# Where the largest entry of a weight strip is taken over the partitions: by a library call on GpSimd, or through DRAM and VectorE

## The chip, the cores and the metric

The kernel runs on one core of one Trainium2 chip. The metric is the time of one execution in microseconds of the device, as the median of several runs. The core has five engines that run side by side, each with its own queue of instructions in a fixed order: TensorE (PE, with its weight loads shown apart as PEld), VectorE (DVE), ScalarE (ACT), GpSimd (POOL) and SyncE (SP), which in this kernel issues most of the transfers. The engines wait for each other by semaphores, and an instruction that waits holds up all that stand behind it on its engine.

## The reference

One inference step of a decoder with two layers, width 1024, on 1040 prompt positions (16 of them meta tokens) and 8 single new tokens. Cut to what matters:

```python
def trunk(x, ...):
    for i in range(2):
        h = rms_norm(x, norm_mix_pre[i])
        m = ssd_mixer(h, ...) if i == 0 else rglru_mixer(h, ...)
        x = x + rms_norm(m, norm_mix_post[i])
        h = rms_norm(x, norm_ffn_pre[i])
        x = x + rms_norm((relu(h @ w1[i]) ** 2) @ w2[i], norm_ffn_post[i])

def ssd_chunked(xdt, a, Bm, Cm, h0, chunk):      # 8 groups of 4 heads of 64, state 128
    cb = einsum("bclgn,bcsgn->bcgls", Cc, Bc)
    scores = cb[:, :, :, None] * Lmat            # Lmat = exp(segment sums), lower triangle
    y_diag = einsum("bcgrls,bcsgrp->bclgrp", scores, x)
    chunk_states = einsum("bcsgn,bcsgrp->bcgrpn", Bc, x * decay_to_end[..., None])
    ...                                          # scan over the chunks, y_off, states out
```

`ssd_mixer` stands between `w_in` (1024 x 6176) and `w_out` (2048 x 1024), `rglru_mixer` between 1024 x 2048 and 1024 x 1024, and each feed-forward part has a `w1` of 1024 x 4096 and a `w2` of 4096 x 1024. All inputs and outputs are float32.

## The kernel before

Everything is kept with the features on the 128 partitions and the tokens along the free axis, in three pieces of about 350 tokens. A product of float32 matrices is made of three float16 products: weights and activations are each split into a high and a low half. For that a weight has to be scaled first by a power of two that comes from its largest entry, and this is done in the kernel, strip by strip.

**The strips.** The weights arrive in strips of 128 partitions x 2048 float32 (1 MB each), 109 of which are scaled as follows. `wlane` (L400) is a generator that issues the load of strip i+1 (`load_strip`, L258, two buffers) and then converts strip i (`wconv`, L286): the largest absolute value of each partition goes to `rm` (128 x 1; on ScalarE for the strips of kind "a", on VectorE for the others), `strip_scale` (L263) makes one number of the 128 and a power of two from it, and `split` (L272) writes the two float16 halves into `wh`, ScalarE the high one, VectorE the low one. Strips of the kinds "H" and "S" (feed-forward) also need sums of their quarters: `sums` (L350) first splits three quarters into `wp` and then lets GpSimd add quarters in place (`ws<-ws`). In `strip_scale` the maximum over the partitions is one GpSimd call, `partition_all_reduce`, which leaves it in all 128 partitions of `wgb`; behind it VectorE makes the power of two in three operations on 128 x 1 (`qw`, `pw`, `sw`, in `pow2`, L246) and its inverse (`winv`). The profile shows 105 of the 109 calls; two more calls of the kind, for other small tables, stay as they are.

**The stages**, in the times of the profiled execution: the start (0 to 133 us: inputs, first norm, first strips; its order is held by hand as written), the eight groups of the state-space layer (`ssd_group`, L985, some 95 us each, to 880 us), its output product (to 1100), the first feed-forward part (to 1715), the recurrent layer (to 2130), and the second feed-forward part, whose last product with the output ends at 2886 us.

**Feed-forward.** Three of the four blocks of `w1` and of `w2` are multiplied by a scheme with seven products of quarters in place of eight (`unit`, L1342). The products of a unit land in four PSUM tiles, and while PE makes the next, VectorE adds them up in an SBUF tile `z`. In front of the products stand sums of the right-hand quarters: for the input `input_sums` (L1324, tiles `f`, written to `TT`), for the hidden layer `square` (L1231) and `t_sums` (L1311): ScalarE squares, GpSimd makes four sums in place (`z<-z`, or `r<-r`), ScalarE and VectorE split them into `HT`. So in the feed-forward GpSimd has two kinds of work in one queue: sums for the activations (`z`, `f`), on which PE's next products depend, and the maxima and sums of the coming weight strips (`wgb`, `ws`).

**State-space groups.** Per group nine chunks are worked off in a loop (L1124): `spread` (L1012) issues, on SP, the broadcast of the cumulative sums (`L<-csd`) and of their exponentials (`ex<-esd`), `pe_a` (L1004) puts three transposes and the product of B and C into one PSUM tile `tp`, `ew_a` (L1026) reads that tile (VectorE: `xdt`, `xdd`, `cbm`; ScalarE: the copy `Bt`) and makes the decay matrix `L`, `pe_b` (L1046) multiplies, and `ew_b` (L1062) gathers. `tri` is the mask of the lower triangle.

**What sets the order.** The program is written as interleaved generators (`tick` lets each lane run one step), and a scheduler then orders each engine's queue, from its own costs and from which tiles' buffers come free. Only the start is held in the written order. Nearly every operation goes through one helper, so most rows of the profile carry its line, L89 (L92 in the start); operations are told apart by their tiles.

Of the kernel before, what the change touches and what calls it, by code (L numbers as in the profile page):

```python
# [10 lines left out]
F32 = mybir.dt.float32  # L11
# [3 lines left out]
OP = mybir.AluOpType  # L15
AX = mybir.AxisListType
PSUM = bass.MemoryType.PSUM
DRAM = bass.MemoryType.DRAM
RED = bass.bass_isa.ReduceOp
EXPSET = "natural_log_exp_and_others"  # L20

P = 128
# [95 lines left out]
class Body:  # L118
# [34 lines left out]
    def setup(self):  # L153
        nc, tc, ctx = self.nc, self.tc, self.ctx
        self.const = ctx.enter_context(tc.tile_pool(name="const", bufs=1))
        self.tiny = ctx.enter_context(tc.tile_pool(name="tiny", bufs=3))
        self.upool = ctx.enter_context(tc.tile_pool(name="u", bufs=1))
        self.ws = ctx.enter_context(tc.tile_pool(name="ws", bufs=2))
        self.wh = ctx.enter_context(tc.tile_pool(name="wh", bufs=5))
# [30 lines left out]
        gb = c.tile([P, 5], F32, name="gb")  # L190
# [18 lines left out]
        self.yd = [self.dram.tile([P, 4 * NV], F16, name=f"yd{i}") for i in range(G)]  # L209
        self.csd = self.dram.tile([288, P], F32, name="csd")  # L210
        self.esd = self.dram.tile([288, P], F32, name="esd")
        self.bcd = [self.dram.tile([8, 2, P], F32, name=f"bcd{i}") for i in range(2)]
        self.mad = [self.dram.tile([P, KT * w], F32, name=f"mad{c}") for c, w in enumerate(WC)]
        a = self.a
# [46 lines left out]
        return st  # L261

    def strip_scale(self, gmax):  # L263
        nc, ty = self.nc, self.tiny
        gb = ty.tile([P, 1], F32, tag="wgb", name="wgb")
        nc.gpsimd.partition_all_reduce(gb, gmax, P, RED.absmax)
        s, p = self.pow2(gb, 1, ty, "w")
        inv = ty.tile([P, 1], F32, tag="winv", name="winv", bufs=8)
        nc.vector.tensor_scalar(inv, p, 2.0 ** -14, None, op0=OP.mult)
        return s, inv, gb  # L270
# [714 lines left out]
    def ssd_group(self, g):  # L985
        nc, v, psp, tmp = self.nc, self.v, self.psp, self.tmp
# [5 lines left out]
        ident, tri = self.ident, self.tri  # L992
# [6 lines left out]
        def dims(i):  # L999
            if i == 0:  # L1000
                return 16, 8, slice(32, 48), 8
            return 128, i - 1, slice(48 + 128 * (i - 1), 176 + 128 * (i - 1)), 24 + 128 * (i - 1)
# [23 lines left out]
        def ew_a(i, tp):  # L1026
            Q, tt, es, _ = dims(i)
            xdt = tmp.tile([P, 4, 64], F32, tag="xdt", name="xdt", bufs=2)
            xdd = tmp.tile([P, 4, 64], F32, tag="xdd", name="xdd", bufs=2)
            L = S.pop(("L", i))  # L1030
            for h in range(4):
                nc.scalar.activation(L[:Q, h, :Q], L[:Q, h, :Q], AF.Relu, scale=-1.0,
                                     bias=self.cs[:Q, tt, 4 * g + h:4 * g + h + 1])
            self.tab(L[:Q, :, :Q], L[:Q, :, :Q], AF.Exp, scale=-1.0)
            tv = tp[:Q, :256].rearrange("p (h d) -> p h d", h=4)
            nc.vector.tensor_tensor(xdt[:Q], tv, self.dt[:Q, tt, hs, None].to_broadcast([Q, 4, 64]), op=OP.mult)
            nc.vector.tensor_tensor(xdd[:Q], tv, self.dtd[:Q, tt, hs, None].to_broadcast([Q, 4, 64]), op=OP.mult)
            Bt = tmp.tile([P, 128], F32, tag="Bt", name="Bt", bufs=2)
            nc.scalar.activation(Bt[:Q], tp[:Q, 256:384], AF.Copy)
            cbm = tmp.tile([P, 128], F32, tag="cbm", name="cbm", bufs=2)  # L1040
            nc.vector.tensor_tensor(cbm[:Q, :Q], tp[:Q, 384:384 + Q], tri[:Q, :Q], op=OP.mult)
            nc.vector.tensor_tensor(L[:Q, :, :Q], L[:Q, :, :Q], cbm[:Q, None, :Q].to_broadcast([Q, 4, Q]),
                                    op=OP.mult)
            S[i] = xdt, xdd, L, Bt
# [79 lines left out]
        for i in range(n + 1):  # L1124
            if i + 1 < n:
                spread(i + 1)
            if i:
                rb = pe_b(i - 1)
            if i < n:
                ra = pe_a(i)  # L1130
            if i:
                ew_b(i - 1, *rb)
            if i < n:
                ew_a(i, ra)
            if i == 1:
                sample_bc()
                sample_a()
            if i in (3, 4, 5, 6):
                sample_b(i - 3)
            if i == 8:  # L1140
                sample_c()
            yield
# [508 lines left out]
```

## Time and profile before

| | |
|---|---|
| median of 3 runs | 2877.12 us (2875.55 to 2878.47) |
| the profiled execution, its own time | 2887.62 us |
| its span in the trace | 2885.9 us |
| mean granted clock of TensorE | 0.96 |
| PE busy | 2571.2 us (89%), 23193 matmuls |
| VectorE busy | 2050.4 us (71%) |
| ScalarE busy | 1403.1 us (49%) |
| GpSimd busy | 743.0 us (26%) |
| transfers | 237.71 MB, 82 GB/s in the mean |

How to read it: the profiled execution is 10.5 us longer than the median of the runs, and 1.7 us of its time lie outside the span. Busy time is time in which an instruction of the engine runs; an instruction that waits for a semaphore is not busy. In a timeline each row has the start (us from the span's start), the busy time of the instructions it stands for, the engine, the line, the operation with its output and inputs, and in brackets how long the engine was idle just before and what ended that. In the list of waits the three numbers are the total, the number of times and the longest, in us. "issue" as a releaser means that the engine waited for nothing that the profile shows. A view by windows gives, for each stretch, its length, the busy time of each engine with the number of instructions, the granted clock of TensorE (1.00 is full speed), the share of the transfer engines and the GB/s moved.

### The profile page before, as it was taken

To read this page: it belongs to the slowest core of one execution; us is meant where nothing else is said; L and a number is where in the kernel's file an instruction comes from. 1 tells how busy PE (TensorE), PEld (TensorE's weight loads), DVE (VectorE), ACT (ScalarE), POOL (GpSimd) and SP (SyncE) were. 2 spreads that over 40 slices of the span, in tenths; PEclk is the share of its full clock that TensorE was granted. 3 is DMA by queue.
4 is the path that set the end of the run, shared out by engine and by line. 5 is a ranking of instruction groups with operands and counts; after the bars stand their busy time and mean duration, and the time that the engine had idled before them with its cause. 6 is when DMAs were issued, how large, how long until landed. Compare 5 with 4: busy or idle time off the path is not lost. (4 is left out here: it accounts for less than half of the span.)

```text
span 2885.9 us, 57203 instructions
## 1 busy us (share of the span) xinstructions
PE 2571.2 (89%) x23193; PEld 2025.2 (70%) x23193; DVE 2050.4 (71%) x4682; ACT 1403.1 (49%) x2436; POOL 743.0 (26%) x1036
## 2 busy tenths in 40 slices
PE   4988998899897999878989999988999879989998
PEld 2655665565565666777988986665666879979976
DVE  4878666766862596567878788787695567777776
ACT  4666565665654355335244253567564335244342
POOL 2233222212222103543232210223012543231201
PEclk9999999999999999989999999999999989999999
DMA  3333233223344330011112122210130011111122
GB/s 125 96 119 127 73 127 119 97 93 119 125 151 164 132 144 30 30 34 42 60 60 89 45 96 96 96 68 33 70 124 30 31 45 45 45 45 45 60 72 93
DMA packets 71496, 237.71 MB, mean 82 GB/s; under 512 B 11120, under 2 KB 37152, under 8 KB 50368
## 3 DMA queue, kind: packets, MB, share of 16 engines
q1 hardware_dynamic: 64848, 199.35, 20.3%
q0 software_dynamic: 6384, 34.71, 3.1%
q8 instruction: 181, 2.97, 0.4%
q14 instruction: 83, 0.68, 0.1%
HBM read 194.67 MB, written 39.36 MB: 81 GB/s over the span
## 5 line engine op out<-in xcount | busy, mean ns | idle before, releaser
L89 PEld LDWEIGHTS <-wh 128*128 128x128 f16 x17040 | 1499.2, 99 | 516.3 <-issue 59.8
L89 PE MATMUL mm<-U,wh 128*128 128x350 f16 (+3 forms) x7056 | 993.2, 297 | 20.1 <-ACT rr L89 10.2
L89 PE MATMUL mm<-H,wh 128*128 128x175 f16 (+5 forms) x5664 | 557.4, 253 | 37.0 <-DVE z L89 33.0
L89 PEld LDWEIGHTS <-wp 128*128 128x128 f16 x3888 | 310.8, 99 | 91.1 <-issue 63.9
L89 POOL TENSOR_TENSOR ws<-ws 128x256 f32<-128x256 f32 (+1 forms) x192 | 205.0, 1068 | 328.7 <-DVE wp L89 214.2
L89 DVE TENSOR_TENSOR z<-z,mm 128x175 f32<-128x175 f32 (+3 forms) x648 | 228.4, 370 | 28.9 <-ACT z L89 22.0
L89 POOL PARTITION_ALL_REDUCE wgb<-rm x100 | 50.3, 503 | 683.2 <-issue 296.6
L89 PE MATMUL mm<-U,wp 128*128 128x175 f16 (+1 forms) x1728 | 154.8, 245 | 56.0 <-DVE z L89 51.9
L89 PE MATMUL mm<-TT,wh 128*128 128x175 f16 (+1 forms) x1728 | 164.7, 246 | 9.8 <-ACT TT L89 8.9
L89 ACT ACTIVATE z<-z,ti 128x700 f32<-128x700 f32 (+1 forms) x72 | 63.0, 875 | 184.7 <-DVE z L89 184.7
L89 DVE SCALAR_TENSOR_TENSOR wh<-ws,sw,wh 128x1024 f16<-128x1024 f32 x94 | 127.0, 1368 | 34.0 <-ACT wh L89 34.0
L89 DVE TENSOR_SCALAR qw<-wgb 128x1 f32<-128x1 f32 x103 | 15.5, 151 | 187.0 <-POOL wgb L89 187.0
L89 ACT ACTIVATE L<-L,cs 128x128 f32<-128x128 f32 (+1 forms) x288 | 92.3, 380 | 109.2 <-DMA L<-csd 90.2
L89 DVE SCALAR_TENSOR_TENSOR conv<-pre,ssmall,conv 128x1072 f32<-128x1072 f32 x78 | 120.3, 1543 | 9.6 <-ACT conv L89 9.2
L89 DVE SCALAR_TENSOR_TENSOR wh<-ws,s,wh 128x256 f16<-128x256 f32 x256 | 114.6, 490 | 11.1 <-ACT wh L89 11.1
L89 PE MATMUL mm<-H,wp 128*128 128x175 f16 (+1 forms) x864 | 91.3, 243 | 27.8 <-DVE z L89 22.5
L89 DVE TENSOR_REDUCE rm<-ws 128x1 f32<-128x2048 f32 x40 | 91.3, 2282 | 28.4 <-DMA ws<-w 24.5
L89 ACT ACTIVATE wh<-ws,sw 128x2048 f16<-128x2048 f32 x47 | 93.7, 1995 | 34.6 <-DVE sw L89 27.8
L89 ACT ACTIVATE wh<-ws,s 128x512 f16<-128x512 f32 x128 | 83.0, 710 | 48.6 <-POOL ws L89 23.4
L89 DVE TENSOR_TENSOR ss<-ss,sqt 128x350 f32<-128x350 f32 (+3 forms) x154 | 75.8, 499 | 41.9 <-ACT sqt L89 41.5
L89 DVE TENSOR_TENSOR H<-z,H 128x175 f16<-128x175 f32 (+5 forms) x120 | 82.5, 705 | 22.5 <-ACT H L89 18.4
L89 POOL TENSOR_TENSOR yf<-yf,ex 128x256 f32<-128x256 f32 x64 | 51.4, 803 | 177.4 <-issue 86.1
(274 smaller groups left out, 4134.6 us busy)
## 6 DMA issues: line engine op xcount, KB each, us to landing
ws<-w SPq DMA_DIRECT2D x64, 1024.0 KB, 4.9
ws<-w_ssd_in SPq DMA_DIRECT2D x24, 1024.0 KB, 5.0
L<-csd SPq DMA_DIRECT2D x64, 256.0 KB, 3.5
ws<-w_lru_in SPq DMA_DIRECT2D x12, 1024.0 KB, 5.1
xd<-xc POOLq DMA_DIRECT2D x6, 1400.0 KB, 5.1
xc<-xd SPq DMA_DIRECT2D x6, 1400.0 KB, 5.9
h<-ssd_h SPq DMA_DIRECT2D x8, 1024.0 KB, 5.3
ex<-esd SPq DMA_DIRECT2D x128, 64.0 KB, 3.9
```

What stands on the lines that cost most here:

```text
L89: r = f(*args, **kw)
```

## The change

In `strip_scale` the GpSimd call is replaced by four steps: SP writes `rm` (128 numbers) to one of four small DRAM tensors `mxd`; SP reads it back as a row of 128 that is broadcast to all partitions (`wrow`, 128 x 128, one buffer); VectorE takes the maximum along the row into `wgb`; the rest follows as before. The pool of the small tiles has 2 buffers in place of 3 (among them `rm` and `wgb`). In `ew_a` VectorE's `cbm` now stands ahead of ScalarE's `Bt`; both read the same PSUM tile `tp`.

```diff
-        self.tiny = ctx.enter_context(tc.tile_pool(name="tiny", bufs=3))
+        self.tiny = ctx.enter_context(tc.tile_pool(name="tiny", bufs=2))
...
+        self.mxd = [self.dram.tile([P, 1], F32, name=f"mxd{i}") for i in range(4)]
+        self.nmax = 0
...
     def strip_scale(self, gmax):
         nc, ty = self.nc, self.tiny
+        d = self.mxd[self.nmax % 4]
+        self.nmax += 1
+        nc.sync.dma_start(d, gmax)
+        row = ty.tile([P, P], F32, tag="wrow", name="wrow", bufs=1)
+        nc.sync.dma_start(row, d.rearrange("p o -> o p").to_broadcast([P, P]))
         gb = ty.tile([P, 1], F32, tag="wgb", name="wgb")
-        nc.gpsimd.partition_all_reduce(gb, gmax, P, RED.absmax)
+        nc.vector.tensor_reduce(gb, row, axis=AX.X, op=OP.max)
         s, p = self.pow2(gb, 1, ty, "w")
...
             nc.vector.tensor_tensor(xdd[:Q], tv, self.dtd[:Q, tt, hs, None].to_broadcast([Q, 4, 64]), op=OP.mult)
+            cbm = tmp.tile([P, 128], F32, tag="cbm", name="cbm", bufs=2)
+            nc.vector.tensor_tensor(cbm[:Q, :Q], tp[:Q, 384:384 + Q], tri[:Q, :Q], op=OP.mult)
             Bt = tmp.tile([P, 128], F32, tag="Bt", name="Bt", bufs=2)
             nc.scalar.activation(Bt[:Q], tp[:Q, 256:384], AF.Copy)
-            cbm = tmp.tile([P, 128], F32, tag="cbm", name="cbm", bufs=2)
-            nc.vector.tensor_tensor(cbm[:Q, :Q], tp[:Q, 384:384 + Q], tri[:Q, :Q], op=OP.mult)
```

The scheduler then orders all queues anew. Three places show what moves. The first is GpSimd's queue in the first feed-forward part, at the first hidden blocks: `ws` are the sums of a strip's quarters, `wgb` the maximum, `z` the sums for the hidden layer. Before:

```order
L89 TENSOR_TENSOR ws<-ws 128x4x128 x4
L89 ISA
L89 ISA wgb<-rm 128x1
L89 ISA
L89 TENSOR_TENSOR z<-z 128x175 x8
L89 TENSOR_TENSOR z<-z 128x174 x4
L89 TENSOR_TENSOR ws<-ws 128x4x128 x4
L89 TENSOR_TENSOR z<-z 128x175 x4
```

And with the change:

```order
L89 TENSOR_TENSOR ws<-ws 128x4x128 x4
L89 TENSOR_TENSOR z<-z 128x175 x8
L89 TENSOR_TENSOR z<-z 128x174 x4
L89 TENSOR_TENSOR ws<-ws 128x4x128 x4
L89 TENSOR_TENSOR z<-z 128x175 x8
L89 TENSOR_TENSOR z<-z 128x174 x4
L89 TENSOR_TENSOR ws<-ws 128x2x128 x16
L89 TENSOR_TENSOR ws<-ws 128x4x128 x12
```

The call and the two nameless instructions at its sides are gone from all 109 places, so that sums follow sums; GpSimd's queue goes from 852 rows to 503.

The second place is VectorE's queue in the first feed-forward part at a strip of `w2`: `rm` is the strip's maximum by partition, `qw` the first operation behind the maximum over the partitions, `z` and `H` work for the products. Before:

```order
L89 TENSOR_TENSOR H<-z,H 128x2x350
L89 TENSOR_TENSOR z<-mm,z 128x2x175
L89 TENSOR_TENSOR r4s<-r_14617,rj 128x4
L89 TENSOR_TENSOR z<-z,mm 128x175
L89 TENSOR_REDUCE rm<-r4s 128x1
L89 TENSOR_TENSOR z<-z,mm 128x2x175
L89 TENSOR_TENSOR z<-z,mm 128x175
L89 TENSOR_TENSOR z<-z,mm 128x174
L89 TENSOR_SCALAR qw<-wgb 128x1
```

And with the change:

```order
L89 TENSOR_TENSOR H<-z,H 128x2x350
L89 TENSOR_REDUCE rm<-r4s 128x1
L89 TENSOR_TENSOR z<-mm,z 128x2x175
L89 TENSOR_TENSOR z<-z,mm 128x175
L89 TENSOR_TENSOR z<-z,mm 128x2x175
L89 TENSOR_TENSOR z<-z,mm 128x175
L89 TENSOR_REDUCE wgb<-wrow 128x1
L89 TENSOR_SCALAR qw<-wgb 128x1
```

Four operations stand between `rm` and the next step, which is now a reduction that waits for a transfer; before it were three, and the wait was for GpSimd.

The third place is SP's queue in a group of the state-space layer: `ws<-w_ssd_in` are strip loads, `L<-csd` and `ex<-esd` the broadcasts for the chunks, `bcd` and `bc` a round trip through DRAM that both kernels have. Before:

```order
L260 DMA ws<-w_ssd_in 128x2048
L1023 DMA ex<-esd 64x2x128 x2
L1018 DMA L<-csd 128x512
L260 DMA ws<-w_ssd_in 128x2048 x2
L1023 DMA ex<-esd 64x2x128 x2
L1018 DMA L<-csd 128x512 x2
L1087 DMA bcd_145<-row 8x256
L1090 DMA bc<-bcd_145 128x2048
```

And with the change:

```order
L1004 DMA h_4154<-ssd_h 128x2048
L262 DMA ws<-w_ssd_in 128x2048
L1026 DMA L<-csd 16x4x16
L1031 DMA ex<-esd 64x2x128 x2
L1026 DMA L<-csd 128x512
L270 DMA mxd_146<-rm 128x1
L1031 DMA ex<-esd 64x2x128 x2
L272 DMA wrow<-mxd_146 128x128
L262 DMA ws<-w_ssd_in 128x2048 x2
L1026 DMA L<-csd 128x512 x2
```

The write and the read of each strip's maximum stand between the broadcasts and ahead of the next strips' loads; SP's queue goes from 217 rows to 518. VectorE's goes from 3825 to 3955.

## The prediction

> **What bounds the kernel now.** The page's first part, its chain of work and one of its costliest groups come first.
>
> ```profile
> PE 2571.2 (89%) x23193; PEld 2025.2 (70%) x23193; DVE 2050.4 (71%) x4682; ACT 1403.1 (49%) x2436; POOL 743.0 (26%) x1036
> ...
> DVE 7%; issue 4%; PE 4%; DMA 2%; ACT 1%; POOL 1%; DVEq 0%; SPq 0%; POOLq 0%; ACTq 0%
> ...
> L89 POOL PARTITION_ALL_REDUCE wgb<-rm x100 | 50.3, 503 | 683.2 <-issue 296.6 <-DVE rm L89 200.7 <-ACT rstd L89 53.0
> ```
>
> PE is busy for 89% of the span, so some 315 us are left in which it is not. GpSimd is busy for 26%, and yet it matters: a maximum over the partitions runs 503 ns, but 296.6 us of idle time before these calls are "issue", time for which the profile shows no cause. The waits say how that is spread.
>
> ```profile
> POOL wgb L89 <- issue: 296.6, 48, 9.4
> ...
> DVE qw L89 <- POOL wgb L89: 187.0, 75, 11.2
> ...
> PE mm L89 <- DVE z L89: 113.1, 70, 6.2
> ...
> POOL ws L89 <- issue: 96.8, 14, 10.3
> ...
> POOL yf L89 <- issue: 86.1, 12, 7.6
> ...
> POOL f L89 <- issue: 56.8, 8, 7.7
> ```
>
> 48 calls stand behind 6.2 us each (296.6/48), and ordinary sums behind a call (`ws`, `yf`, `f`) behind 6.9, 7.2 and 7.1 us. GpSimd seems to change its code on the way into the call and on the way back: 13 us for half a microsecond of work. Whether PE feels it is seen in a feed-forward place in the timeline:
>
> ```profile
> 1472.46 0.41 POOL L89 PARTITION_ALL_REDUCE wgb<-rm  x1 [6.10 <-issue]
> 1472.90 0.15 DVE L89 TENSOR_SCALAR qw<-wgb 128x1 f32<-128x1 f32 x1 [4.49 <-POOL wgb L89]
> 1473.85 1.08 PE L89 MATMUL mm<-U,wp 128*128 128x175 f16 x12 [1.50 <-DVE z L89]
> ...
> 1479.64 4.08 POOL L89 TENSOR_TENSOR z<-z 128x175 f32<-128x175 f32 x8 [6.78 <-DVE wh L89]
> ...
> 1486.14 0.33 DVE L89 TENSOR_TENSOR z<-z,mm 128x175 f32<-128x175 f32 x1
> 1486.52 1.90 PE L89 MATMUL mm<-U,wp 128*128 128x174 f16 x12 [5.81 <-DVE z L89]
> ```
>
> VectorE stands 4.49 us at `qw`, which costs PE 1.50. The way back costs more: the sums of `z` start 6.78 us after the call (put down to `wh`, but the same length as "issue" above), `z` comes late, PE stands 5.81 us. There are 14 such places, where GpSimd goes from a call straight to sums of `z` or `f`. Cut out as windows, the first, the last and the sum of the 14; then of four stretches between them in which everything runs:
>
> ```profile
> 1198.00:1220.00 22.00, 15.34 (x164) 14.58 (x162) 14.31 (x43) 7.21 (x13) 10.59 (x16) 0.77 0.14 50
> ...
> 2577.00:2596.00 19.00, 15.21 (x178) 14.72 (x176) 15.98 (x38) 9.10 (x19) 8.26 (x13) 0.91 0.16 57
> sum 281.00, PE 197.83 PEld 190.14 DVE 200.26 ACT 109.31 POOL 132.18; mean PE 14.13 PEld 13.58 DVE 14.30 ACT 7.81 POOL 9.44
> ```
>
> ```profile
> 1345.00:1470.00 125.00, 119.76 (x1553) 117.57 (x1551) 99.42 (x256) 40.76 (x77) 27.65 (x29) 1.00 0.15 52
> ...
> 2600.00:2720.00 120.00, 115.58 (x1500) 113.60 (x1498) 96.21 (x250) 38.85 (x74) 26.26 (x28) 1.00 0.16 54
> sum 435.00, PE 419.01 PEld 411.00 DVE 345.76 ACT 137.80 POOL 100.05; mean PE 104.75 PEld 102.75 DVE 86.44 ACT 34.45 POOL 25.01
> ```
>
> The 14 have PE at 70% (197.83/281), with a granted clock of 0.77 in the first and 0.91 in the last, the four at 96% and 1.00. Idle PE is paid twice, by the gap and by the lower clock behind it. In the four, PE makes a matmul in 0.080 us (125/1553, 120/1500).
>
> **The change part by part.** The sum is made against the profiled execution, 2887.6 us; its median scale lies 10.5 us lower.
>
> *Code changes in the feed-forward: −75.* With all 109 calls gone, sums follow sums. Ends: at the pace of the four stretches the 14 would be over in 175 us, as 2183 matmuls (all fourteen counts added) times 0.080; that is 106 less. At the other end stands 45, two fifths of the 113.1 us that PE waits for `z`: the sums themselves (4.08 us for eight) and the steps behind them stay. In between: PE idles 83 us in the 14 (281 − 197.83), and at the four's rate (16 in 435) 10 would stay. I take that difference and a little of the clock, 75.
>
> *The round trip in the call's place.* Its price is in no row, since no such transfer runs now; near rows are these, two with times from the timeline, three with their median time to landing.
>
> ```profile
> 416.54 0.29 SPq L1087 DMA_DIRECT2D bcd<-row  x1
> 417.85 0.33 SPq L1090 DMA_DIRECT2D bc<-bcd  x1
> ```
>
> ```profile
> ex<-esd SPq DMA_DIRECT2D x128, 64.0 KB, 3.9
> ...
> csd<-dtt SPq DMA_DIRECT2D x1, 144.0 KB, 2.5
> ...
> L<-csd SPq DMA_DIRECT2D x8, 4.0 KB, 2.5
> ```
>
> SP issues `bc`, which has to wait for `bcd`'s landing, 1.3 us after it, and `csd` took 2.5: the write costs 1.3 to 2.5, I take 2.0 as about the middle. The read brings 64 KB as 128 rows of 512 B, like `ex`; alone in the queue it should be nearer to the small `L` (2.5) than to 3.9 behind a neighbour: 2.8. With 0.5 for hand-offs and the reduction: 5.3 us, between 4.1 (1.3+2.5+0.3) and 7.0 (2.5+3.9+0.6). The Trainium skill ("DMA: Bandwidth & Descriptors", "Anatomy of one DMA — SWDGE (gpsimd) path") puts a fixed 2.0 us on each transfer plus bytes at 436 GB/s; by it, as an estimate, the trip is 2.0 + 2.15 + 0.5 = 4.65 us, the 14 in the next term fall away, and the time is 2785. The 3.9 of `ex` is far above that rule's 2.15, so the rows keep the sum.
>
> *New waits: +8.* VectorE stops at the reduction of `wrow` until the read has landed, and behind it in its queue stand the sums of `z` that free PE's banks. What it does in the meantime has these prices:
>
> ```profile
> L89 DVE TENSOR_TENSOR z<-z,mm 128x175 f32<-128x175 f32 x336 | 106.3, 329 | 3.4 <-ACT z L89 2.3
> L89 DVE TENSOR_TENSOR z<-z,mm 128x350 f32<-128x350 f32 x96 | 49.2, 512 | 3.4
> ...
> DVE qw L89 <- POOL wgb L89: 68.0, 23, 5.8
> ```
>
> At the strip of `w2` in the order the cover is two operations of each size, 1.7 us. In the place above a stop of 4.49 became 1.50 at PE: 3.0 us are hidden by matmuls already fed. So 5.3 − 1.7 − 3.0 = 0.6 us at 24 such strips is 14; where the cover is longer nothing is left. Against it go the waits for `wgb` of today (last row: 68.0 us in 23 waits in the first feed-forward part alone, 3.0 each, so at PE only the long ones count), some 6. Net +8; ends 0 (trip 4.1) and +25 (trip 7.0: 2.3 at 24, less 30 that hit longer covers or go with today's waits).
>
> *Start: −6.* Nothing here is hidden, the order being held.
>
> ```profile
> 17.26 0.40 POOL L89 PARTITION_ALL_REDUCE wgb<-rm  x1 [7.20 <-DVE rm L92]
> ...
> 24.99 3.77 POOL L92 TENSOR_TENSOR U<-uf,U 128x1400 f16<-128x1400 f32 x1 [7.33 <-issue]
> 28.81 1.62 PE L92 MATMUL mm<-U,wh 128*128 128x350 f16 x5 [6.65 <-POOL U L92]
> ```
>
> ```profile
> 48.96 1.54 PE L92 MATMUL mm<-ss,ones 128*128 128x350 f32 x2 [11.74 <-POOL ss L92]
> ```
>
> ```profile
> 15.00:20.00 5.00, 1.53 (x2) 0.50 (x2) 4.39 (x9) 2.79 (x3) 0.40 (x1) 1.00 1.04 402
> 20.00:25.00 5.00, 0.45 (x1) 0.21 (x2) 5.00 (x8) 4.37 (x4) 0.01 (x1) 1.00 0.10 28
> ```
>
> Two waits of PE, 6.65 and 11.74, each hold one way back of some 7 us, which goes. But the first maximum, ready at 17.3, meets transfers that fill the engines to about 21, so its power of two slips from 17.7 to about 24. Ends −12 and +4; I take −6.
>
> *Recurrent layer: −5*, from 0 to the 10.2 us below, part of whose inputs come from GpSimd. *State-space groups: 0, from −25 to +30.*
>
> ```profile
> PE mm L89 <- ACT rr L89: 10.2, 4, 4.8
> ...
> DVE cbm L89 <- ACT Bt L89: 28.0, 23, 3.1
> ```
>
> ```profile
> SPq L1018 <- DVE L L89: 178.2, 37, 11.9
> ```
>
> For it: the 86.1 us of `yf`, and `cbm` no longer waits for `Bt` (28.0), with one hand-off less on the way to `L`; `Bt` comes a `cbm` later in exchange, and PE's state product with it. Against it: SP stands at each read until its write has landed, 1.3 to 2.5 us, with the chunks' broadcasts behind it, and at the write until `rm` is there. The broadcasts wait on SP for their own buffers (178.2 us) already, so most of that lies beside it. 24 strips times one microsecond either way gives about ±25. The reductions (between 0.18 us, a 64-wide one below, and twice that, 109 times, 20 to 39 us of VectorE, which is 79% busy in the smooth stretches, 345.76/435) hide in its slack; if that cover goes, up to 39.
>
> ```profile
> L89 DVE TENSOR_REDUCE bx<-small 128x1 f32<-128x64 f32 (+1 forms) x2 | 0.4, 177 | 0.0
> ```
>
> Two buffers for small tiles cost nothing: their readers finish a strip before the next but one.
>
> Sum: −75 + 8 − 6 − 5 + 0 = −78, so 2809.6 as profiled, **2799** on the median's scale. Its own range, from the ends of the terms taken together by squares (30, 17, 10, 5, 30 and 15 for the reductions, 49 in all): about 2750 to 2848.
>
> **The rivals.** *Half comes back (0.14).* With the calls gone PE waits instead for the rest of that chain, squares, four sums, split, sum of products: for it speaks that 4.08 us of sums lie between 1479.64 and PE's start at 1486.52; against it, that PE stays at 96% where the same sums run without a call. Then two fifths of the 75 are left, −30, and the other terms cancel: 2847.
>
> *Slower, the round trip is too long (0.09).* VectorE's stop then shows not at a few long waits but at all 64 strips of the feed-forward. With an average cover of 2.9 us between `rm` and the reduction and 3.0 hidden at PE, a trip of t costs 64 (t − 5.9). Against the 86 us that the other terms bring (75, 6 and 5), it decides from 7.3 us on; at 8.0 it is +134 − 86 = +48: 2925. Against it: the longest sum of rows is 7.0, and each strip's write finds quiet engines (share 0.15), since its own load has landed.
>
> *Slower, the gaps have another cause (0.07).* If GpSimd's 7 us are not a code change but, say, a wait that the trace misses, they stay; the call itself took 0.44 us from its start to `qw` (1472.46 to 1472.90) where it came at once, and a trip of 5.3 takes its place: the 14 worked out above and some 6 at other strips, +20, so 2897. The Trainium skill ("GPSIMD Engine Reference", "4.1 Engine selection") gives reductions along the partitions to GpSimd and not to VectorE; here VectorE reduces only along the free axis, and the DRAM does the turn. Against it: 6 to 7 us show in four kinds of rows above. It is also the case in which the change does not do what it says.
>
> *No change (0.04).* Gains and new waits cancel: 2877.
>
> **How the numbers follow.** Forecast 0.66, half 0.14, long trip 0.09, other cause 0.07, no change 0.04. A measurement can tell about 0.2%, 5.8 us, from no change; so faster 0.66 + 0.14 = 0.80, same 0.04, slower 0.16. The range holds the forecast's own and the half: 2750 to 2870; the cases left out have 0.20.
>
> **What would show it.** Right: GpSimd's rows on "issue" all but gone, PE near 96% and clock 1.00 at the first hidden blocks, PE's wait for `z` under 60 us, `qw` no longer waiting but the reduction of `wgb` for about 2 us a strip. Wrong: 6 to 7 us gaps before GpSimd's sums as before (other cause); the reduction waiting over 4 us at most strips with PE waiting for `z` behind it (long trip); SP's broadcasts landing later and PE waiting for `L` (state-space groups).

## The result, and the profile after

The changed kernel takes 3321.57 us (median of 4 runs, 3315.7 to 3332.05) against 2876.44 for the kernel before on the same chip: a ratio of 1.155, interval 1.1519 to 1.1582. It is 445 us slower where the prediction said 78 faster. The page of the profiled execution, its first line, the chain's shares by engine and by line, and one group:

```profile
span 3317.2 us, 57335 instructions
PE 2662.2 (80%) x23193; PEld 2103.3 (63%) x23193; DVE 2063.4 (62%) x4791; ACT 1400.0 (42%) x2436; POOL 710.4 (21%) x927
...
DMA 5%; DVE 3%; PE 2%; issue 1%; ACT 0%; DVEq 0%; SPq 0%; ACTq 0%
PE mm L89 2%; DMA mxd<-rm 2%; DMA wrow<-mxd 1%; DMA ws<-w 1%; DVE z L89 1%; DVE wh L89 0%; DVE U L89 0%; DVE r L89 0%; DVE rm L89 0%; DVE ss L89 0%; DVE H L89 0%; ACT sqt L89 0%; DVE xc L89 0%; DVE acc L89 0%; ACT z L89 0%
...
L89 DVE TENSOR_REDUCE wgb<-wrow 128x1 f32<-128x128 f32 x103 | 29.3, 284 | 707.4 <-DMA wrow<-mxd 707.4
```

PE is at 80% for 89, and the two new transfers are now in the chain that ends last. Of the 431 us by which the span is longer, 91 lie in PE's own busy time (2662.2 for 2571.2), with a mean granted clock of 0.91 for 0.96; the rest is idle time of PE. The reduction itself is cheap (284 ns), but VectorE was idle for 707.4 us in front of it. The waits come next, then SP's own wait, then how long the two transfers take from issue to landing (medians of those whose landing is known):

```profile
DVE wgb L89 <- DMA wrow<-mxd: 707.4, 83, 14.9
...
PE mm L89 <- DVE z L89: 244.2, 77, 11.4
POOL ws L89 <- issue: 201.5, 17, 22.4
...
PE mm L89 <- DVE pw L89: 83.3, 16, 6.9
```

```profile
SPq L272 <- DMA mxd<-rm: 782.7, 96, 15.0
```

```profile
wrow<-mxd SPq DMA_DIRECT2D x109, 64.0 KB, 5.0
...
mxd<-rm SPq DMA_DIRECT2D x105, 0.5 KB, 8.3
```

SP stands in front of the read until the write has landed, 8.2 us each time (782.7/96), and VectorE in front of the reduction, 8.5 us (707.4/83). One strip in the smooth part of the first feed-forward, where PE had been at 96%:

```profile
1520.49 2.29 DVE L89 TENSOR_REDUCE rm<-ws 128x1 f32<-128x2048 f32 x1 [1.80 <-DMA ws<-w]
...
1522.80 0.32 SPq L270 DMA_DIRECT2D mxd<-rm  x1
...
1530.05 0.62 PE L89 MATMUL mm<-HT,wh 128*128 128x175 f16 x6
1530.34 0.32 SPq L272 DMA_DIRECT2D wrow<-mxd  x1
1535.63 0.28 DVE L89 TENSOR_REDUCE wgb<-wrow 128x1 f32<-128x128 f32 x1 [9.71 <-DMA wrow<-mxd]
...
1536.83 1.06 PE L89 MATMUL mm<-H,wh 128*128 128x175 f16 x6 [6.16 <-DVE pw L89]
```

The trip (the write and the read, from the write's issue to the reduction) took 12.8 us here: 7.5 for the write, 5.3 for the read. VectorE ran out of other work 9.71 us before its end; PE, whose banks VectorE has to empty, stood 6.16 us, and its next six matmuls took 1.06 us where six took 0.62 before the stop. Over the strips behind the state-space groups the medians are 8.5 for the write and 4.9 for the read, 13.4 together. The same stretches of matmuls that were two of the four smooth ones (125 us each for 1553 and 1573 matmuls) now take 160 and 170 us:

```profile
1452.00:1612.00 160.00, 130.00 (x1559) 128.23 (x1558) 99.30 (x255) 40.12 (x75) 27.66 (x28) 0.91 0.13 43
2722.00:2892.00 170.00, 132.33 (x1570) 130.69 (x1568) 102.44 (x267) 41.76 (x80) 27.68 (x28) 0.89 0.12 41
```

### The profile page after: what moved, and what is told of

Same layout as the page of the kernel before. It is cut to its first block, busy times and chain, and to the rows that moved or that the text cites. A ratio compares the mean times of both kernels' runs of the same rounds, so it can differ in the third digit from the quotient of the medians.

```text
span 3317.2 us, 57335 instructions
## 1 busy us (share of the span) xinstructions
PE 2662.2 (80%) x23193; PEld 2103.3 (63%) x23193; DVE 2063.4 (62%) x4791; ACT 1400.0 (42%) x2436; POOL 710.4 (21%) x927
## 5 line engine op out<-in xcount | busy, mean ns | idle before, releaser
L89 PEld LDWEIGHTS <-wh 128*128 128x128 f16 x17040 | 1557.8, 101 | 690.1 <-issue 128.8
L89 PE MATMUL mm<-U,wh 128*128 128x350 f16 (+3 forms) x7056 | 1003.5, 300 | 101.6 <-DVE z L89 31.2
L89 PE MATMUL mm<-H,wh 128*128 128x175 f16 (+5 forms) x5664 | 585.1, 261 | 102.9 <-DVE pw L89 62.2
L89 DVE TENSOR_REDUCE wgb<-wrow 128x1 f32<-128x128 f32 x103 | 29.3, 284 | 707.4 <-DMA wrow<-mxd 707.4
L89 PEld LDWEIGHTS <-wp 128*128 128x128 f16 x3888 | 323.9, 101 | 195.1 <-issue 191.8
L89 PE MATMUL mm<-U,wp 128*128 128x175 f16 (+1 forms) x1728 | 164.9, 253 | 137.8 <-DVE z L89 132.7
L89 PE MATMUL mm<-TT,wh 128*128 128x175 f16 (+1 forms) x1728 | 174.1, 255 | 0.0
L89 DVE SCALAR_TENSOR_TENSOR wh<-ws,s,wh 128x256 f16<-128x256 f32 x256 | 115.2, 495 | 13.8 <-ACT wh L89 13.8
L89 ACT ACTIVATE wp<-ws,sq 128x512 f16<-128x512 f32 x72 | 48.5, 711 | 161.8 <-DVE sh L89 83.2
L89 ACT ACTIVATE wp<-ws,s 128x128 f16<-128x128 f32 x144 | 48.2, 389 | 154.5 <-issue 84.7
L89 ACT ACTIVATE H<-z 128x700 f16<-128x700 f32 (+1 forms) x96 | 64.7, 674 | 103.2 <-POOL z L89 101.5
```

The lines of the kernel that those rows point to most:

```text
L89: r = f(*args, **kw)
```

## The experiments

The ratios are to the kernel before, on the same chip in the same hours (2872.88 to 2877.34 us).

**Which part of the change costs.** One kernel has only the way through DRAM, one only the new order of `cbm` and `Bt`, one all but the two buffers. The first is the changed kernel with the lines of `cbm` and `Bt` put back and the pool with three buffers, the second the kernel before with those lines exchanged, the third the changed kernel with

```diff
-        self.tiny = ctx.enter_context(tc.tile_pool(name="tiny", bufs=2))
+        self.tiny = ctx.enter_context(tc.tile_pool(name="tiny", bufs=3))
```

> The changed kernel with cbm and Bt in their old order and three buffers for the small tiles again, so that only the maximum's way through DRAM is left of the change. Theory (the round trip of some 13 us stops VectorE and with it PE): 3320 us, within 15. Rival (the reordered reads of the transposes' bank or the fewer buffers cost part of it): 3280 or less.

> The kernel before with cbm read ahead of Bt and nothing else changed. Theory: no effect beyond 10 us either way, 2867 to 2887 us. Rival (Bt, now later, holds up PE's state product in 72 chunks): 2895 us or more, with PE's wait for Bt well above the 29.5 us of before.

> The changed kernel with three buffers for the small tiles again, its cbm still ahead of Bt. It was 43 us slower than the kernel without both. If the two buffers cost that (rm and its followers now wait for the trip two strips back): 3265 to 3285 us. If the order of cbm and Bt costs it: 3310 us or more.

Measured: 3278.22 us (1.1411, 1.1392 to 1.143); 2839.87 us (0.9884, 0.9869 to 0.9899); 3251.92 us (1.1288, 1.125 to 1.1326). By its number the first goes to the rival: the way through DRAM is 405 us of the loss (3278 − 2873), nine tenths, and the other two edits add 43 to it. The third buffer saves 70 us in the changed kernel (3322 to 3252), a little more than expected of it. The new order of `cbm` and `Bt` is a gain, 33 us by itself, against both expectations; beside the way through DRAM it is 26 (3278 to 3252; 35 by the ratios, since the two ran on different chips).

**What the call had cost.** Kernels that do without the call's result: a maximum by a matmul, and the maximum left out, each also with the call still made. The matmul:

```diff
-        nc.gpsimd.partition_all_reduce(gb, gmax, P, RED.absmax)
+        ps = self.mm()
+        nc.tensor.matmul(ps[:, :P], gmax.to_broadcast([P, P]), self.ident, start=True, stop=True)
+        nc.vector.tensor_reduce(gb, ps[:, :P], axis=AX.X, op=OP.max)
```

or, with the maximum left out, so that each partition has a scale of its own,

```diff
-        nc.gpsimd.partition_all_reduce(gb, gmax, P, RED.absmax)
+        nc.vector.tensor_copy(gb, gmax)
```

and for the calls that nobody waits for, in each of the two, also

```diff
+        gx = ty.tile([P, 1], F32, tag="wgx", name="wgx")
+        nc.gpsimd.partition_all_reduce(gx, gmax, P, RED.absmax)
```

A fifth has the maximum left out and `cbm` ahead of `Bt`.

> The kernel before with neither GpSimd's call nor the way through DRAM: one matmul with rm as the weights, broadcast along the columns, and the identity as the moving side puts the 128 maxima as a row into all partitions of a PSUM bank, and VectorE reduces that. Theory of the prediction (the call's code changes on GpSimd cost PE 75 to 90 us): 2780 to 2810 us. Rival (those gaps have another cause, and the call was nearly free): 2860 to 2890 us.

> As the kernel with the maximum by a matmul, but GpSimd still makes its 109 calls, into a small tile that nobody reads. If PE's gaps in the feed-forward come from GpSimd's code changes, which make the sums of z and f late: back to 2860 to 2880 us. If they come from VectorE's wait for the call's result: about as fast as without the calls, 2780 to 2810 us.

> The kernel before with the maximum over the partitions left out: VectorE copies rm into wgb, so that each partition has a scale of its own; no call on GpSimd, no transfer, nothing to wait for. Theory of the prediction (the calls' code changes cost PE some 75 us in the feed-forward and more in the start): 2770 to 2810 us. Rival (only the state-space groups gain, as with the maximum by a matmul, where they were 53 us shorter): 2815 to 2840 us.

> As the kernel with the maximum left out, but GpSimd makes its 109 calls into a tile that nobody reads. Code-change theory: 60 to 90 us above the kernel without them. Rival (what the calls cost is VectorE's wait for their result): within 15 us of it.

> As the kernel with the maximum left out, with cbm read ahead of Bt. If the 33 us that this order gained by itself come from the hand-off between ScalarE and VectorE: 25 to 40 us below the kernel with the maximum left out. If they come from where the scheduler put GpSimd's calls after it (sums of yf waited 86 us on issue before, 15 us then): within 10 us of it.

Measured: 2915.36 us (1.0143, 1.0128 to 1.0158) and 3076.56 us (1.0704, 1.0685 to 1.0723) with the matmul; 2674.62 us (0.9294, 0.9271 to 0.9317), 2823.27 us (0.9816, 0.9796 to 0.9835) and 2682.01 us (0.9323, 0.9297 to 0.9349) without a maximum. The kernel with the maximum by a matmul fits neither side. In it VectorE waits for that matmul behind PE's products (39.6 us in 24 waits), and PE waits for the strips' halves; here are two of PE's waits, neither of which is among the rows of the kernel before:

```profile
PE mm L89 <- ACT wh L89: 89.0, 39, 7.9
PE mm L89 <- DVE wh L89: 80.2, 87, 1.9
```

Why that costs so much was not followed further; the idle calls on top of it cost 161. The pair with the maximum left out is the clean one: 109 calls whose result nobody waits for cost 149 us (2823 − 2675), and the call and the wait for it together 203. Both are more than was expected (2770 to 2810 us without the maximum, 60 to 90 for the idle calls). The rows of that kernel with the idle calls, then of the one without:

```profile
POOL wgx L89 <- issue: 118.0, 19, 7.5
...
POOL yf L89 <- issue: 93.6, 12, 8.9
...
PE mm L89 <- DVE z L89: 86.1, 32, 7.2
...
POOL f L89 <- issue: 56.7, 8, 7.6
POOL z L89 <- issue: 56.0, 8, 7.2
```

```profile
POOL ws L89 <- issue: 131.3, 15, 14.3
...
PE mm L89 <- DVE z L89: 41.6, 42, 2.0
```

With the calls, sums of `yf`, `f` and `z` stand 7 to 8 us on "issue" behind them and PE waits for `z` up to 7.2 us at a time; without, PE's longest is 2.0 and those issue waits are not among the rows. So these gaps were the calls' own, which the third rival had doubted. The row of `ws` is another matter: it stays where there are no calls (131.3 us, and 201.5 in the changed kernel). In each of its 15 waits without calls, and in 12 of the 14 before the change, `ws` starts 0.13 to 0.15 us behind VectorE's last `wp`, so what it waited for is the split, and the prediction read this row wrongly as a change of code. The order of `cbm` and `Bt` gains nothing where there are no calls: 7 us more, inside the intervals. In the kernel with that order alone, the sums of `yf` had waited on issue only

```profile
POOL yf L89 <- issue: 15.0, 2, 7.5
```

against 86.1 before. That speaks for where the scheduler put the calls after the edit, away from `yf`, as the source of most of the 33 us, and not for the hand-off's 28.0; it was not tested by itself. What the gain beside the way through DRAM is made of stays open.

**What makes the trip long.** The write as four rows of 128 bytes, and (with `mxd` 128 x 128) as 128 rows of 512; the second reads back the first row alone and so leaves the maximum out:

```diff
-        nc.sync.dma_start(d, gmax)
+        t32 = ty.tile([P, 32], F32, tag="wt32", name="wt32")
+        nc.vector.transpose(t32, gmax.to_broadcast([P, 32]))
+        nc.sync.dma_start(d.rearrange("(q i) o -> q (i o)", q=4), t32[0::32])
```

```diff
-        nc.sync.dma_start(d, gmax)
...
+        nc.vector.tensor_copy(wide, gmax.to_broadcast([P, P]))
+        nc.sync.dma_start(d, wide)
...
-        nc.sync.dma_start(row, d.rearrange("p o -> o p").to_broadcast([P, P]))
+        nc.sync.dma_start(row, d[0:1].to_broadcast([P, P]))
```

> The changed kernel with the write to DRAM made of four rows of 32 numbers: VectorE first turns rm into rows, 32 partitions at a time, and SP writes one row of each; the read is as it was. Theory (128 pieces of 4 bytes are what makes the write take 8 us; four rows take some 2): trip 7.5 us, and 64 strips times 6 us less, 2920 to 2980 us. Rival (any such write takes about 8 us, and the trip stays): 3300 us or more.

> The changed kernel with the write widened: VectorE repeats rm 128 times along the row, and SP writes 128 rows of 512 bytes in place of 128 pieces of 4 bytes; the read takes the first row, so the maximum over the partitions is left out. If the size of the pieces makes the write long: write to read under 4 us and 2740 to 2850 us. If their number does (128 against the 4 rows of the fast variant): write to read 7 us or more and 3250 us or more.

Measured: 2729.71 us (0.9488, 0.9457 to 0.9519) and 2744.59 us (0.9538, 0.9498 to 0.9579). A strip of the first in the feed-forward, then one of the second:

```profile
1363.59 0.50 SPq L272 DMA_DIRECT2D mxd<-wt  x1
...
1365.22 0.32 SPq L274 DMA_DIRECT2D wrow<-mxd  x1
...
1368.04 0.29 DVE L89 TENSOR_REDUCE wgb<-wrow 128x1 f32<-128x128 f32 x1
```

```profile
1375.84 0.32 SPq L272 DMA_DIRECT2D mxd<-wwide  x1
...
1377.42 0.32 SPq L274 DMA_DIRECT2D wrow<-mxd  x1
...
1380.55 0.29 DVE L89 TENSOR_REDUCE wgb<-wrow 128x1 f32<-128x128 f32 x1 [0.29 <-DMA wrow<-mxd]
```

And the second's two transfers, from issue to landing:

```profile
mxd<-wwide SPq DMA_DIRECT2D x109, 64.0 KB, 1.7
wrow<-mxd SPq DMA_DIRECT2D x109, 64.0 KB, 2.8
```

Write to read is 1.6 us in both; read to reduction 2.8 and 3.1, with VectorE hardly standing at these two strips. The number of pieces is not what makes the write long: 128 rows of 512 bytes land as fast as four of 128, while 128 pieces of 4 bytes take 8.5. What is left is their size, or that all 128 fall into the same 512 bytes of DRAM, where the rows of 512 lie apart; no run separates the two. Both the trip (4.5 us for an expected 7.5) and the time (2730 for 2920 to 2980) came out below what the theory had said. With the fast write the changed kernel is the fastest of all that leave nothing out (with two or with three buffers, 2730 us), 5.1% below the kernel before; the write's form alone is worth 592 us (3322 to 2730).

**How a long trip costs.** The next kernels hold the reduction back by hand, or lengthen the fast trip by copies (hops) from DRAM to DRAM, which the scheduler counts. In the first `strip_scale` becomes a generator, and its reduction is issued after VectorE's last instruction of that moment (`late` is set once the start is over); in the others the second edit stands once or three times behind the write of four rows; a last one has four rows and three buffers for the small tiles.

```diff
+        for _ in range(3 if self.late else 0):
+            yield
         gb = ty.tile([P, 1], F32, tag="wgb", name="wgb")
+        if self.late:
+            nc.vector.prev = nc.vector.last
         nc.vector.tensor_reduce(gb, row, axis=AX.X, op=OP.max)
+        if self.late:
+            nc.vector.prev = None
```

```diff
+            nc.sync.dma_start(e.rearrange("(q i) o -> q (i o)", q=4), d.rearrange("(q i) o -> q (i o)", q=4))
+            d = e
```

> The changed kernel with the reduction of wrow held back on VectorE behind more of the other work (three steps of the interleaved generators later, behind the instruction of VectorE written last). By the queue's order and the durations of before the cover in the feed-forward and recurrent strips goes from 5.0 to 13.7 us in the mean, and the sum of what a trip of 13.4 us leaves over cover and 3.0 us from 518 to 339. Theory (PE is lost to VectorE standing at the reduction): 3110 to 3190 us. Rival (the strips themselves come too late, so that any delay in the chain costs): 3300 us or more.

> The fast trip (four rows written) with one more hop: SP copies the 128 numbers from one DRAM tensor to another before they are read back, some 2.3 us more, trip about 6.9 us; the scheduler counts the hop and puts a little more of VectorE's other work ahead of the reduction (median 5.6 us for 4.4). Theory (PE loses what the trip leaves over that cover and 3.0 us at each strip): the sum goes from 11 to 38, so 2750 to 2775 us. Rival (every microsecond of delay in a strip's chain costs alike, 592 us for 8.8 us of trip between the fast and the slow one): 2730 + 67 times 2.3, 2860 to 2900 us.

> The fast trip with three more hops, trip about 11.5 us, nearly as long as the changed kernel's 13.4; but the scheduler counts the hops and puts the reduction behind 11.5 us of VectorE's other work (median; 4.1 in the changed kernel). Theory (VectorE standing uncovered is what costs): the sum over cover and 3.0 us is 126 for 11, so 2820 to 2870 us. Rival (the length of the trip itself costs, since the strips come late): 3100 us or more.

> The fast trip with three buffers for the small tiles, one for the turned rows. If the 70 us that the two buffers cost in the changed kernel come from the long trip holding rm and its followers: within 15 us of 2730 us, little below it at most. If two buffers cost something of their own: 2690 us or less.

Measured: 3337.58 us (1.1602, 1.1574 to 1.1629); 2775.44 us (0.9666, 0.9652 to 0.9681); 2800.26 us (0.975, 0.9731 to 0.9768); 2730.06 us (0.9496, 0.9478 to 0.9514). By its number the first falls to its rival, but it overshot and decides nothing: the reduction came a whole strip late, 26 us behind its read, and PE waited for the halves instead, by its rows:

```profile
PE mm L89 <- ACT wh L89: 206.5, 55, 11.1
PE mm L89 <- ACT wp L89: 148.2, 42, 7.5
```

The hops say more. With three of them it is 7.9 us from the write to the read again, nearly as in the changed kernel, and with 2.9 for the read the trip is 10.8; but the scheduler counts hops, where it gave the slow write no more room than the fast one. Counted in the traces, from `rm` on VectorE to the reduction, the changed kernel has 3.3 us of other work in the median, the one with four rows 3.4, and the one with three hops 9.7 (the expectations, worked out from the queue's order and the durations of before, had 4.1, 4.4 and 11.5). VectorE's wait with four rows, with one hop and with three, then a strip of the last:

```profile
DVE wgb L89 <- DMA wrow<-mxd: 149.8, 56, 8.1
```

```profile
DVE wgb L89 <- DMA wrow<-mxe: 141.4, 63, 7.3
```

```profile
DVE wgb L89 <- DMA wrow<-mxe: 230.5, 63, 14.8
```

```profile
1392.82 0.53 SPq L273 DMA_DIRECT2D mxd<-wt  x1
...
1395.32 0.48 SPq L276 DMA_DIRECT2D mxe<-mxd  x1
...
1397.11 2.24 SPq L276 DMA_DIRECT2D mxe<-mxe  x2
...
1400.67 0.32 SPq L279 DMA_DIRECT2D wrow<-mxe  x1
...
1404.83 0.29 DVE L89 TENSOR_REDUCE wgb<-wrow 128x1 f32<-128x128 f32 x1 [2.79 <-DMA wrow<-mxe]
```

VectorE stands 230.5 us for 707.4 and the kernel takes 2800 us, better than the first theory's 2820 to 2870 and far from the 3100 of the rival. With one hop (trip 6.4) it is 2775, the theory's upper end; a trip of 6.4, had every microsecond cost alike, would have made it 2857 (67 for each of 1.9). So most of the loss comes from a reduction that the queue reaches long before its data. Not all of it: with one hop VectorE stood no longer than with none (141.4 us for 149.8), and the kernel still lost 46 us, with PE waiting for `z` 106 times for 63; why was not looked into. And the two buffers cost nothing at the short trip (2730.06 to 2729.71); the 70 us hang on the long one.

**Without GpSimd and without DRAM.** One more kernel has `cbm` ahead of `Bt` and takes the maximum on VectorE alone, by copies, a reduction, four turns and a reduction:

```diff
...
+        for q in range(4):
+            nc.vector.tensor_copy(c4[:, q:q + 1], gmax[32 * q:32 * q + 32])
...
+        nc.vector.tensor_reduce(m32, c4, axis=AX.X, op=OP.max)
...
+        for q in range(4):
+            nc.vector.transpose(t32[32 * q:32 * q + 32], m32.to_broadcast([32, 32]))
+        nc.vector.tensor_reduce(gb, t32, axis=AX.X, op=OP.max)
```

> The kernel before with cbm ahead of Bt and the maximum over the partitions made by VectorE alone: four copies bring the quarters of rm side by side on 32 partitions, a reduction, four 32 x 32 transposes back to all partitions, a reduction; ten small operations, neither GpSimd nor a transfer. Theory (the chain costs about 1.5 us in VectorE's queue and VectorE has slack): 2690 to 2720 us, ahead of the fast trip's 2730. Rival (109 times 1.5 us on VectorE, which is busy 79% in the smooth stretches, delay the sums of products): 2760 us or more.

Measured: 2757.77 us (0.9587, 0.9561 to 0.9613), at the rival's edge: 4.1% below the kernel before, and 28 us behind the four rows through DRAM.

## Why the prediction was wrong

The time by stages, cut at the same matmul in each trace (us, worked out from the traces; the columns are the kernel before, the changed one, the one with the maximum left out, that one with idle calls, and the one with four rows; the last phase ends with the last matmul):

| stage | before | changed | left out | idle calls | four rows |
|---|---|---|---|---|---|
| start | 133 | 155 | 123 | 134 | 128 |
| state-space groups | 747 | 764 | 699 | 737 | 701 |
| their output product | 220 | 257 | 206 | 213 | 207 |
| first feed-forward | 615 | 761 | 548 | 590 | 562 |
| recurrent layer | 445 | 519 | 436 | 450 | 451 |
| second feed-forward | 630 | 764 | 564 | 605 | 576 |
| last phase | 87 | 90 | 88 | 87 | 88 |

**The step that failed is the price of the round trip**, "the write costs 1.3 to 2.5, I take 2.0". It cost 8.5, and the read after it 4.9 for 2.8: 13.4 us in place of 5.3, outside the stated 4.1 to 7.0. The near rows were a write of 8 KB in 8 pieces of 1 KB and one of 144 KB in pieces of 512 bytes; that this one has pieces of 4 bytes was not asked for, and so the upper bound was set by rows that could not show it. The Trainium skill ("DMA: Bandwidth & Descriptors", "Specifications") says that below 512 bytes the transfer engine does a read-modify-write; in these runs rows of 128 bytes cost nothing extra (1.6 us as with 512), so the limit is not seen there, but the direction is that of the 4-byte pieces; whether this is what makes them slow, no run here shows. The forecast had cited the Trainium skill's fixed 2.0 us ("Anatomy of one DMA — SWDGE (gpsimd) path" on the same page), which this write exceeds fourfold; that section is about transfers that GpSimd issues, and these two are issued by SP, so it did not promise them that price.

**The rival that ended slower was the right one.** Its mechanism, VectorE stopping at nearly every strip, is what the waits show: it stood before 52 of the 54 reductions that fall into the two feed-forward parts, before 51 of them for more than 4 us. Its formula, at a trip that it had not thought possible, gives 64 (13.4 − 5.9) − 86 = +394 us, against 445 measured, but that nearness is in part luck: without the gains at the start and in the recurrent layer (6 and 5) it gives +405 for the feed-forward parts, where 280 were lost (761 + 764 less 615 + 630), and the other stages, for which it has a gain of 11, lost some 150. Its chance of 0.09 rested on "the longest sum of rows is 7.0". In the trace PE is idle 646 us, 314 of these while VectorE stands at the reduction, 404 with the two microseconds behind each stop; in the kernel with the maximum left out it is idle 158.

**Code changes, −75:** the mechanism was right (of GpSimd's waits on "issue" the changed kernel has hardly any left but those of `ws`) and the size too small for the whole program. In the two feed-forward parts idle calls cost 83 us (590 + 605 less 548 + 564), near the 75; the wait for the call's result, for which the prediction had allowed 6, costs 50 more there (615 + 630 less 590 + 605). The 6 came from the rule that a wait of VectorE below 3 us costs PE nothing; what that rule misses was not tested.

**New waits, +8:** 413 us in the two feed-forward parts (761 + 764 less 548 + 564). With the trip of 4.5 that four rows give it is 26 (562 + 576 less 1112). That is near the +25 of the term's upper end by luck, since at 4.5 the term's own rule leaves nothing (4.5 − 1.7 − 3.0 is below 0).

**Start, −6:** +22, by the same trip; with four rows −5. The order held by hand lets ScalarE stand for the scale, and all behind it with it: three waits of up to 13.8 us in the changed kernel, four of up to 7.1 before.

```profile
ACT wh L92 <- DVE winv L92: 36.8, 3, 13.8
```

**Recurrent layer, −5:** +74 and, with four rows, +6. **State-space groups, 0:** +17; with four rows −46, a gain that the range of −25 did not hold; 38 of the 48 that leaving out the maximum gives there are the calls (737 less 699). Their output product, for which there was no term, lost 37 and would have gained 13. **Two buffers, nothing:** 70 us at the long trip; which of the small tiles is taken too long was not looked into. **Reductions of `wrow`:** 29.3 us of VectorE in all, within the 20 to 39 that were named; what they cost PE by themselves no run separates.

With a trip near the forecast one (4.5 for 5.3) the time is below the forecast and its range: 2730 for 2799.

## What to carry to other kernels

Before a value goes through DRAM, look how it lies: one number per partition is 128 pieces of 4 bytes, and here that took five times as long as the same bytes in four rows (8.5 to 1.6 us); a 32 x 32 turn on VectorE in front of the write was worth 592 us. A transfer's price is read from a row with pieces of the same size, and where no row has such pieces, the bound is open upwards and the rival that hangs on it deserves more than what is left over. An engine that waits in order stands with everything behind it: most of what a wait cost here is the trip less the work that the queue has ahead of it, so the order has to know the trip's true length, as with the three hops.

## What the hardware showed beyond that

The slow write hardly occupies the transfer engines. In windows over the strip shown above (1522.80 to the read's issue at 1530.3) there is a share of 0.08 in the first microsecond, with 1 GB/s, and nothing in the next four:

```profile
1522.80:1523.80 1.00, 1.00 (x17) 0.96 (x15) 0.86 (x3) 0.94 (x2) 0.00 (x0) 1.00 0.08 1
1523.80:1527.80 4.00, 4.00 (x56) 4.00 (x54) 2.08 (x5) 0.00 (x0) 0.00 (x0) 1.00 0.00 0
```

The time lies between the packets and the news of their landing; what fills it, no trace here shows. Over the strips behind the state-space groups the write's last packet starts 1.0 us after its issue in the median (1.2 with four rows), while the read that waits for the landing is issued 8.5 us after it (1.6). The read of a row just written in 4-byte pieces was slower too (4.9 us against 2.9 with four rows, the same 128 rows of 512 bytes), and its first packet starts 2.9 us after its issue for 1.0. Other transfers are held up as well: in the changed kernel seven stores of 54 KB by GpSimd (`ssd_conv_o`), each issued 3.1 to 4.3 us behind such a write, landed after 6.2 to 9.9 us, where the eight before the change took 2.4 to 4.5. And a GpSimd call costs where its result is not used: 149 us for 109 calls (the profile before shows all 109, 105 from `rm` and 4 from `gmx`), 1.4 us each on PE's side, where a call between two sums takes GpSimd some 13 us.
